# Routing on un-normed tokens, with the first expert's weights split before a branch, in a two-block float32 kernel

## The chip, the core and the metric

The kernel runs on one core of a Trainium2 chip. A core has TensorE (PE, matrix products; its weight loads are shown as PEld), VectorE (DVE), ScalarE (ACT), GpSimd (POOL) and SyncE (SP, which issues all the DMAs of this kernel). Each engine works through its own list of instructions in order and waits on semaphores for the others. The metric is the device time of one execution in microseconds (us).

## The reference, cut to what matters

A batch of one sequence of 256 tokens of 1024 float32 values goes through a mixer, a cross attention, a hierarchical mixture of experts (MoE), and then a second stack of two more layers. The change lies between the cross attention and the MoE:

```python
def rmsnorm(x, g):
    xf = x.astype(jnp.float32)
    y = xf * lax.rsqrt(jnp.mean(xf * xf, axis=-1, keepdims=True) + EPS)
    return (y * g.astype(jnp.float32)).astype(x.dtype)
...
    x = x + memory_cross_attention(...)          # ends with o @ w_xo
    x = x + hierarchical_moe(rmsnorm(x, norm_ffn_g[l]), w_rg[l], b_rg[l], w_re[l], b_re[l],
                             w_e_gate[l], w_e_up[l], w_e_down[l])
...
def hierarchical_moe(h, ...):
    p_grp = jax.nn.softmax(t @ w_rg + b_rg, axis=-1)      # 4 groups
    g_val, g_idx = lax.top_k(p_grp, 1)
    le = (t @ w_re + b_re).reshape(n, 4, 4)               # 4 experts in each group
    le_sel = jnp.take_along_axis(le, g_idx[:, :, None], axis=1)[:, 0]
    e_val, e_idx = lax.top_k(jax.nn.softmax(le_sel, axis=-1), 2)
    ...
    act = silu(einsum('nd,edf->nef', t, w_e_gate)) * einsum('nd,edf->nef', t, w_e_up)
    act = act * gate[:, :, None]
    out = einsum('nef,efd->nd', act, w_e_down)
```

Each of the 16 experts has a gate and an up matrix of 1024 x 256 and a down matrix of 256 x 1024.

## The kernel before

Activations lie feature-major: `xT` holds x as 128 partitions (features) x 8 feature tiles x 256 tokens. To keep float32 precision, each weight piece of 128 x 1024 values (512 KB, fetched by `wfetch`, L90, into one of 6 buffers `raw`) is split by `wsplit` (L96): ACT writes a rounded high part `whi` (L99) and DVE the remainder `wlo` (L100); activations have such pairs too (`hTh`/`hTl`, `xgh`/`xgl`). A product then is three matmuls: high by high, high by low, low by high (`mm_fm`, L141 to L143; `mm_tm`, L148 to L150). The split pairs sit in 6 buffers as well, and each is free again when TensorE has used it. PSUM has 8 banks, which `phase` (L58) shares out to kinds of tiles; `bank` (L69) takes one.

The order within an engine is not written out by hand: the recording layer places the instructions of each engine by its own estimate of time, with `fence`/`behind` as hints. Work that waits for another engine is written as generators; `later` queues one and `tick` moves each queued one a step on, after each block of 256 output columns.

The stretch that the change touches runs as follows. The output projection of the attention (`out_proj` with `w_xo`, L356) makes four column blocks of 48 matmuls, called xo blocks 0 to 3 here. After each, `resid` adds it to `xT` (DVE), and `norm.squares` squares it (ACT) and sums the squares over features by matmuls with a matrix of ones (L295). After block 3, `norm.finish` computes 1/rms for all 256 tokens on 128 x 256 values (L225 to L241), multiplies x by it and by the gain, and splits the result into `hTh`/`hTl` (L306 to L314, L217, L218). The router's logits are 24 matmuls over `hT` (L835 to L838). They are copied, transposed to tokens, and get their bias (L844). Then come `first_max` (L900) for the group, the rank of each token within its group by five small matmuls (L915 to L919), the `slot` of each token (L925 to L927), and `over`, which says whether any group has more than 128 tokens. `hT` is transposed to token-major `hMh`/`hMl` by 32 transposes (L936 to L947). `gating` (L952) computes the weights of the two chosen experts. `ada_mm` (L437) are small matmuls for a later layer, 4 for each 512 KB piece, and serve as filler; `ada_load` fetches those pieces.

Then stands a branch on `over` (L1101, L1102): when a group overflows, a whole second MoE pass runs. With these inputs it is skipped, but every engine loads the flag and branches. After the branch, `moe_pass` (L995) builds a 0/1 matrix `Pm` (token to slot, L999) and gathers each group's tokens by matmuls with it: `gather(0)` for groups 0 and 1 before the experts, then `gather(1)` for groups 2 and 3, each of 8 steps of 4 matmuls (L1011) with one ACT copy (L1013) and one DVE copy (L1014). The 16 experts follow, with up to three of them in flight: four pieces of gate and up, 24 matmuls (`gu`), a sigmoid, products on DVE, two transposes, two pieces of down, 12 matmuls (`py`); after every fourth expert a scatter back into `xT` (L1082, L1085). Three of expert 0's four pieces are fetched ahead of the branch (`pre`, L993) and split after it. SP, DVE and ACT are joined at the branch: what follows on one waits for the other's passing it.

Of the kernel before, what the change touches and what calls it, by code (L numbers as in the profile page):

```python
# [30 lines left out]
N_P = 3  # L31
# [8 lines left out]
def two_blocks_kernel(ctx, tc, A, out):  # L40
# [315 lines left out]
    def out_proj(aT, w2d, nx, gate=None, ws=(), ps0=None):  # L356

        for c in range(4):
# [6 lines left out]
            later(resid(c, ps, gate, nx))  # L365
# [133 lines left out]
    with tc.tile_pool(name="kv", bufs=1, reuse_waits="tile") as kvp:  # L499
# [265 lines left out]
        with tc.tile_pool(name="xa", bufs=2, reuse_waits="tile") as xp, tc.tile_pool(name="ad", bufs=B_X, reuse_waits="tile") as ad:  # L765
# [51 lines left out]

            skewed([head(h) for h in range(4)])
            nx = norm(g_ffn)
            wrt = xp.tile([P, KD, 20], F32, name="wrt", bufs=1)  # L820
# [3 lines left out]
            wrth = xp.tile([P, KD, 20], F32R, name="wrth", bufs=1)  # L824
            wrtl = xp.tile([P, KD, 20], F32R, name="wrtl", bufs=1)
            hilo(wrth, wrtl, wrt)
# [3 lines left out]
            out_proj(oT, A["w_xo"][0], nx)  # L830
            drain()
            hT = nx.finish()
            ada_mm(N_X)

            pl = bank("logits")  # L835
            for k in range(KD):
                mm_fm(pl[:20, :S], (wrth[:, k, :], wrtl[:, k, :]), hT, k, 0, k == 0, k == KD - 1, 20)
            lf = xp.tile([20, S], F32, name="lf", bufs=1)  # L838
            SC.activation(lf, pl[:20, :S], AF.Copy)
            pl = bank()  # L840
            for t in range(2):
                T.transpose(pl[:, 20 * t:20 * t + 20], lf[:, t * P:(t + 1) * P], ident[:20, :20])
            L = cp.tile([P, 2, 20], F32, name="L")
            V.tensor_tensor(L, pl[:, :40].rearrange("p (t c) -> p t c", t=2), bc(brt.unsqueeze(1), [2, 20]), op=OP.add)  # L844
# [36 lines left out]
    with (tc.tile_pool(name="ad3", bufs=5, reuse_waits="tile") as ad,  # L881
# [4 lines left out]
        for j in range(4):  # L886
            V.memset(w4[:, j:j + 1], float(4 - j))
            V.memset(b128[:, j:j + 1], float(128 * j))
# [11 lines left out]
        def first_max(l, nm):  # L900
# [8 lines left out]
            V.tensor_tensor(oh, oh, bc(r.unsqueeze(2), [2, 4]), op=OP.is_equal)  # L909
# [9 lines left out]
        T.matmul(pr[:, 8:12], ones, goh[:, 1, :], start=False, stop=True)  # L919
        rk = st([2, 4], "rk")  # L920
# [14 lines left out]

        hM = (mp.tile([P, 2, D], F32R, name="hMh"), mp.tile([P, 2, D], F32R, name="hMl"))  # L936
        for t in range(2):
            for c in range(2):
                for i in range(2):
                    ps = bank()  # L940
                    for j in range(4):
                        fence["T"] = T.transpose(ps[:, j * P:(j + 1) * P], hT[i][:, 4 * c + j, t * P:(t + 1) * P].bitcast(F32), ident)
                    dst = hM[i][:, t, 512 * c:512 * c + 512]
                    if i == 0:
                        SC.activation(dst, ps, AF.Copy)
                    else:
                        V.tensor_copy(dst, ps)  # L947

        drain()
        ada_step(N_R, ad)  # L950

        def gating():  # L952
# [27 lines left out]
            V.tensor_tensor(o1, o1, o2, op=OP.add)  # L980
            return o1


        def gate_up(E, kc):
            return [(lambda r, u=u: r.rearrange("p (k u f) -> p k u f", k=2, u=2)[:, :, u, :],
                     A[nm][0, E, kc * 256:kc * 256 + 256, :].rearrange("(k p) f -> p k f", p=P))
                    for u, nm in enumerate(("w_e_gate", "w_e_up"))]


        pre = []  # L990
        sqb = mp.tile([P, 2, CH], F32, tag="sq", name="pre")
        for kc in range(N_P):
            pre.append(wfetch(gate_up(0, kc), sqb[:, kc, :] if kc < 2 else ad.tile([P, CH], F32, tag="ada", name="pre")))  # L993

        def moe_pass(slot, okm, nx=None, pre=()):  # L995
# [39 lines left out]
            def expert(E):  # L1035
# [4 lines left out]
                for kc in range(4):  # L1040
                    hl = wsplit(pre[kc], CH) if E == 0 and kc < len(pre) else wload(gate_up(E, kc), CH)
                    for k in range(2):
                        wgu.append(tuple(w[:, k * 512:(k + 1) * 512] for w in hl))
# [666 lines left out]
```

## Time and profile before

| what | us |
|---|---|
| median of 3 runs (1231.42 to 1235.02) | 1234.59 |
| the profiled execution | 1230.13 |
| its span in the trace | 1228.1 |
| TensorE busy in the span | 1183.5 |
| VectorE busy | 888.9 |
| ScalarE busy | 696.2 |

The profiled execution is one run; 2.0 us of its time lie outside the span. A busy TensorE is not a TensorE at its peak: matmuls are counted as busy at a lower granted clock too. The granted clock is given as a share of full speed: 1.00 is 2.4 GHz and 0.50 is 1.2 GHz. Times within the span count from its start.

### The profile page before, as it was taken

What the parts mean: (1) busy time and instruction counts of PE and PEld (TensorE: products, weight loads), DVE (VectorE), ACT (ScalarE), POOL (GpSimd) and SP (SyncE); (2) the same over time, 40 slices, a digit from 0 to 9 for tenths busy, and PEclk for the clock granted to TensorE, in tenths of its full rate; (3) what the DMA queues carried; (4) which work ended last, traced back from release to release, by engine and by line L of the source; (5) the groups of instructions that cost most, each with busy time, mean ns of one, the idle gap of its engine ahead of it and who ended that gap; (6) DMA issues with size and microseconds to landing.
All of it is one profiled execution on the core that took longest, in us unless ns stands there. A gap on an engine that the chain in (4) does not pass through costs nothing.

```text
span 1228.1 us, 22512 instructions
## 1 busy us (share of the span) xinstructions
PE 1183.5 (96%) x8762; PEld 1061.1 (86%) x8762; DVE 888.9 (72%) x1672; ACT 696.2 (57%) x1163; POOL 26.6 (2%) x34
## 2 busy tenths in 40 slices
PE   7999999999879999899999999999999989999998
PEld 6989999989657888679757899999977768999998
DVE  7999977664468999888778595577489567654443
ACT  6644447553347887576457475555466455655543
POOL 0000000000000000070000000000000000000000
PEclk9999999999979999999999999999999999999999
DMA  7565575791357999786452597597656246656551
GB/s 240 199 218 185 163 222 174 248 320 58 124 176 256 330 354 350 278 254 206 124 186 92 190 379 250 183 325 267 221 210 191 85 138 207 227 186 190 188 172 35
DMA packets 177551, 257.76 MB, mean 210 GB/s; under 512 B 14239, under 2 KB 138999, under 8 KB 177436
## 3 DMA queue, kind: packets, MB, share of 16 engines
q1 hardware_dynamic: 177436, 256.24, 63.1%
q8 instruction: 71, 1.16, 0.4%
q14 instruction: 44, 0.36, 0.1%
HBM read 255.15 MB, written 1.05 MB: 209 GB/s over the span
## 4 chain that ended last, share of the span: by engine, by line
PE 64%; DVE 3%; ACT 2%; issue 1%; DMA 1%; ACTq 0%; DVEq 0%
PE fm L142 6%; PE fm L143 6%; PE fm L141 6%; PE mo L141 5%; PE mo L142 5%; PE mo L143 5%; PE tm L148 3%; PE tm L150 3%; PE tm L149 3%; PE gu L150 2%; PE gu L148 2%; PE gu L149 2%; PE ada L434 1%; PE o L1449 1%; PE py L148 1%
## 5 line engine op out<-in xcount | busy, mean ns | idle before, releaser
L100 DVE TENSOR_TENSOR wlo<-raw,whi 128x1024 fp32r<-128x1024 f32 (+1 forms) x382 | 455.3, 1213 | 168.0 <-ACT whi L99 163.7
L99 ACT ACTIVATE whi<-raw 128x1024 fp32r<-128x1024 f32 (+1 forms) x382 | 391.9, 1048 | 267.7 <-PE fm L142 139.0
L141 PE MATMUL fm<-hTh,whi 128*128 128x256 f32 (+1 forms) x968 | 272.8, 282 | 3.2 <-ACT hTh L217 3.2
L142 PE MATMUL fm<-hTl,whi 128*128 128x256 f32 (+1 forms) x968 | 272.8, 282 | 1.8 <-DVE hTl L551 0.7
L143 PE MATMUL fm<-hTh,wlo 128*128 128x256 f32 (+1 forms) x968 | 271.7, 281 | 0.8 <-DVE wlo L100 0.8
L141 PEld LDWEIGHTS fm<-hTh,whi 128*128 128x128 f32 (+1 forms) x968 | 182.2, 188 | 5.6 <-ACT hTh L217 4.6
L142 PEld LDWEIGHTS fm<-hTl,whi 128*128 128x128 f32 (+1 forms) x968 | 182.5, 189 | 4.0 <-DVE hTl L218 2.7
L143 PEld LDWEIGHTS fm<-hTh,wlo 128*128 128x128 f32 (+1 forms) x968 | 182.3, 188 | 1.1 <-DVE wlo L100 1.0
L142 PE MATMUL mo<-ul,whi 128*128 128x256 f32 x512 | 142.9, 280 | 0.0
L143 PE MATMUL mo<-uh,wlo 128*128 128x256 f32 x512 | 142.8, 280 | 0.0
L141 PE MATMUL mo<-uh,whi 128*128 128x256 f32 x512 | 141.7, 280 | 0.0
L143 PEld LDWEIGHTS mo<-uh,wlo 128*128 128x128 f32 x512 | 96.2, 188 | 0.0
L142 PEld LDWEIGHTS mo<-ul,whi 128*128 128x128 f32 x512 | 96.2, 188 | 0.0
L141 PEld LDWEIGHTS mo<-uh,whi 128*128 128x128 f32 x512 | 95.4, 188 | 0.4 <-issue 0.4
L148 PE MATMUL tm<-whi,hTh 128*128 128x512 f32 x176 | 69.4, 400 | 0.7 <-ACT hTh L217 0.7
L149 PE MATMUL tm<-wlo,hTh 128*128 128x512 f32 x176 | 69.0, 393 | 0.0
L150 PE MATMUL tm<-whi,hTl 128*128 128x512 f32 x176 | 68.0, 392 | 0.0
L142 PE MATMUL fm<-oTl,whi 128*128 128x256 f32 x192 | 54.4, 286 | 0.9 <-DVE oTl L1621 0.8
L141 PE MATMUL fm<-oTh,whi 128*128 128x256 f32 x192 | 53.1, 284 | 1.4 <-ACT oTh L1620 1.3
L143 PE MATMUL fm<-oTh,wlo 128*128 128x256 f32 x192 | 53.0, 280 | 0.0
L148 PE MATMUL gu<-whi,xgh 128*128 128x512 f32 x128 | 51.1, 401 | 1.8 <-ACT xgh L1013 1.8
L629 DVE SCALAR_TENSOR_TENSOR acv<-apad,chv,acv 128x256 f32<-128x256 f32 x120 | 51.4, 478 | 0.0
(523 smaller groups left out, 2136.9 us busy)
## 6 DMA issues: line engine op xcount, KB each, us to landing
ada<-in_w_ada_dram SPq DMA_DIRECT2D x96, 512.0 KB, 6.1
raw<-in_w_mlp_in_dram SPq DMA_DIRECT2D x64, 512.0 KB, 3.8
raw<-in_w_mlp_out_dram SPq DMA_DIRECT2D x64, 512.0 KB, 4.8
raw<-in_w_in_dram SPq DMA_DIRECT2D x48, 512.0 KB, 3.7
raw<-in_w_e_down_dram SPq DMA_DIRECT2D x32, 512.0 KB, 5.4
raw<-in_w_e_gate_dram SPq DMA_DIRECT2D x61, 256.0 KB, 5.2
raw<-in_w_e_up_dram SPq DMA_DIRECT2D x61, 256.0 KB
raw<-in_diff_w_in_dram SPq DMA_DIRECT2D x24, 512.0 KB, 4.1
```

The source lines that it names most:

```text
L99: behind("A", SC.activation(hi[:, :n], raw[:, :n], AF.Copy))
L100: last["lo"] = behind("V", V.tensor_tensor(lo[:, :n], raw[:, :n], hi[:, :n].bitcast(F32), op=OP.subtract))
L141: T.matmul(ps, whi[:, c:c + ncol], xh[:, xk, :], start=first, stop=False, **kw)
L142: T.matmul(ps, whi[:, c:c + ncol], xl[:, xk, :], start=False, stop=False, **kw)
L143: return T.matmul(ps, wlo[:, c:c + ncol], xh[:, xk, :], start=False, stop=last, **kw)
L148: T.matmul(ps, xh[:, xk, t0:t0 + P], w[0], start=first, stop=False)
L149: T.matmul(ps, xh[:, xk, t0:t0 + P], w[1], start=False, stop=False)
L150: return T.matmul(ps, xl[:, xk, t0:t0 + P], w[0], start=False, stop=last)
L434: behind("T", T.matmul(ada_part["ps"][32 * j:32 * j + 32, :], w, r[:, S * j:S * j + S], start=start, stop=stop, skip_group_check=True))
L629: V.scalar_tensor_tensor(acv[:, f, :], apad[:, f, j:j + S], chv[:, f, j:j + 1], acv[:, f, :], op0=OP.mult, op1=OP.add)
L1449: T.matmul(o_[64 * hp:64 * hp + 64, :], vTM[:, a, s, gi, :], PT[hp, s, a], start=s == 0 and a == 0, stop=False, skip_group_check=True)
```

## The change

- **Router on x instead of its norm.** The gain `norm_ffn_g` is multiplied into the router's weights (`wrt`, now 32 columns wide, plain float32 and not split). Logits, sums of squares and token-major copies of x are taken column block by column block in `resid_r`, one `tick` after each xo block. The 1/rms of a token is then one number per token in token-major form: `inv_rms` on 128 x 2 values, multiplied into the logits (`L`) and into the rows `xM` (x times the gain, token-major) to give `hMh` and `hMl`. The 32 transposes of `hT`, `norm.finish` and the split of the router's weights are gone.
- **Weights.** Expert 0's four pieces, and the high parts of expert 1's first two, are fetched and split ahead of the branch; twelve pieces in all are fetched ahead of it.
- **Order around the branch.** `Pm` is built ahead of the branch, `gating` behind it; 16 filler matmuls (`ada_mm(N_R)`) move behind it. The flag's load on DVE is put behind the last rows of `hMl`. The skip path is asked to be the one that the compare falls through to.
- **2 KB rows.** In a piece of gate and up, a partition now holds two neighbouring rows of the matrix (2 KB in one run) instead of two rows 128 apart (1 KB each); to match, the gather takes every second feature of 256 as a tile (`cs`).
- **Second gather.** The 8 steps of `gather(1)` are spread over experts 0 to 7, one in each.
- The overflow pass has its own weight buffers. Constants `w4` and `b128` are set on POOL.

```diff
-N_P = 3
+N_P = 2
...
+            def resid_r(c, ps, gate, nx):
+                xs = xT[:, 2 * c:2 * c + 2, :]
...
+                yield
+                for k in (2 * c, 2 * c + 1):
+                    T.matmul(lgb[:32, :S], wrt[:, k, :], xT[:, k, :], start=k == 0, stop=k == KD - 1)
+                pz = bank()
+                for f in range(2):
+                    for t in range(2):
+                        T.transpose(pz[:, (2 * t + f) * P:(2 * t + f + 1) * P], xs[:, f, t * P:(t + 1) * P], ident)
...
+                if c >= 2:
+                    for f in range(2):
+                        fence["T"] = T.matmul(ssb[32:64, :S], ones[:, :32], (sq if c == 3 else rq["qs"])[:, f, :],
+                                              start=c == 2 and f == 0, stop=c == 3 and f == 1)
+                V.tensor_tensor(xM[:, :, 256 * c:256 * c + 256], pz.rearrange("p (t d) -> p t d", t=2),
+                                bc(grow[:, 256 * c:256 * c + 256].unsqueeze(1), [2, S]), op=OP.mult)
+
+            out_proj(oT, A["w_xo"][0], None, res=resid_r)
+
+            pre = [wfetch(gate_up(i // 4, i % 4)) for i in range(6)]
+            split0 = [wsplit(r, CH) for r in pre[:4]]
+            pre += [wfetch(gate_up(i // 4, i % 4)) for i in range(6, 10)]
             drain()
-            hT = nx.finish()
-            ada_mm(N_X)
...
+            ada_mm(3)
...
+            rM = inv_rms(pl[:, :, 32], 2, 1.0 / D, "rM", cp)
             L = cp.tile([P, 2, 20], F32, name="L")
-            V.tensor_tensor(L, pl[:, :40].rearrange("p (t c) -> p t c", t=2), bc(brt.unsqueeze(1), [2, 20]), op=OP.add)
+            for t in range(2):
+                V.scalar_tensor_tensor(L[:, t, :], pl[:, t, 0:20], rM[:, t:t + 1], brt, op0=OP.mult, op1=OP.add)
+            ada_mm(N_X - 3)
...
+                SC.activation(hi, xm, AF.Copy, scale=rM[:, t:t + 1])
+
+        def rows_lo(t, c):
+            hi, lo = (v[:, t, 512 * c:512 * c + 512] for v in hM)
+            return V.scalar_tensor_tensor(lo, xM[:, t, 512 * c:512 * c + 512], rM[:, t:t + 1], hi.bitcast(F32),
+                                          op0=OP.mult, op1=OP.subtract)
...
-            gather(0)
+            for d in range(8):
+                gather(0, d)
+            o1, gated = gating()
+            if nx is not None:
+                ada_mm(N_R)
...
+                if E < 8:
+                    gather(1, E)
...
+        Pm, fence["H"] = places(slot, okm, "Pm")
+        for t in range(2):
+            Pm_ins = behind("H", rows_lo(t, 1))
...
-        with tc.If(flag > 0):
+        with tc.If(flag > 0, preferred_fallthrough_block=False):
```

How this moves TensorE's instructions between the last xo block and the branch: before, the sums of squares are followed by 32 filler matmuls, the logits from the normed `hT`, the ranks and the transposes of `hT`. Rows name the line, the operation, what is written and read, and the shape; xN is a repeat.

```order
L143 MATMUL fm<-oTh,wlo 128x256
L295 MATMUL ss<-qs,ones 128x256 x2
L295 MATMUL ss<-sq,ones 128x256 x2
L434 MATMUL ada<-ada,cond 32x256 x32
L141 MATMUL logits<-hTh,wrth 20x256
...
L842 MATMUL ax<-ident,lf 128x20 x2
L915 MATMUL rank<-go,tri 128x4
...
L942 MATMUL ax<-ident,hTh 128x128 x4
...
L434 MATMUL ada<-ada,cond 32x256
L1101 TENSOR_LOAD over
L1102 COMPARE_AND_BRANCH
```

Now, at the same place (the first row is the last matmul of xo block 3):

```order
L143 MATMUL fm<-oTh,wlo 128x256
L856 MATMUL logits<-xT,wrt 32x256 x2
L860 MATMUL ax<-ident,xT 128x128 x4
L867 MATMUL ss<-qs,ones 32x256 x2
L856 MATMUL logits<-xT,wrt 32x256
L860 MATMUL ax<-ident,xT 128x128 x2
...
L867 MATMUL ss<-sq,ones 32x256 x2
L434 MATMUL ada<-ada,cond 32x256 x12
L884 MATMUL ax<-ident,lf 128x64 x2
L434 MATMUL ada<-ada,cond 32x256 x20
L961 MATMUL rank<-go,tri 128x4
```

The logits and transposes of blocks 2 and 3 stand behind the last xo matmul; the same rows for blocks 0 and 1 stand ahead of it, behind blocks 1 and 2. Only `lf` (the logits and sums of squares, copied) and its two transposes lie between the sums and the ranks.

On DVE, from the last `go` (the chosen group) to the branch, the changed kernel has these rows:

```order
L955 TENSOR_TENSOR go<-go,gr 128x8
L976 SCALAR_TENSOR_TENSOR hMl<-xM,ir_y,hMh 128x512 x2
L982 TENSOR_TENSOR rk<-rank,go 128x8
...
L988 TENSOR_TENSOR slot<-slot,rnk 128x2
L491 SCALAR_TENSOR_TENSOR gA<-modc,gcols 128x8
L1038 TENSOR_SCALAR Pm<-slot_i,slot,okm 128x512 x2
L976 SCALAR_TENSOR_TENSOR hMl<-xM,ir_y,hMh 128x512 x2
L1191 TENSOR_TENSOR gfA<-gcols,gA 128x8
L1165 TENSOR_LOAD over
L1169 COMPARE_AND_BRANCH
L1169 UNCONDITIONAL_BRANCH
```

Before, the last rows there were copies of transposed `hT` and `modc`, and `Pm` stood behind the branch. Also a jump still stands right behind the compare.

On DVE right behind the branch, before (`wlo` are splits of weights, `xgl` the gather's copies; all of `gating` stands ahead of the branch):

```order
L491 SCALAR_TENSOR_TENSOR gA<-modc,gcols 128x8
L999 TENSOR_SCALAR Pm<-slot_i,slot,okm 128x512 x2
L1116 TENSOR_TENSOR gfA<-gcols,gA 128x8
L100 TENSOR_TENSOR wlo<-pre,whi 128x1024 x3
L1014 CAST xgl<-ax 128x256 x2
L100 TENSOR_TENSOR wlo<-raw,whi 128x1024 x3
L1014 CAST xgl<-ax 128x256 x2
```

And now, from the third copy of the gather on:

```order
L1025 TENSOR_TENSOR e2o<-e2o,e2m 128x8
L1058 CAST xgl<-ax 128x256
L1026 TENSOR_TENSOR e1o<-e1o,e2o 128x8
L100 TENSOR_TENSOR wlo<-raw,whi 128x1024 x2
L1058 CAST xgl<-ax 128x256
L100 TENSOR_TENSOR wlo<-raw,whi 128x1024
L1058 CAST xgl<-ax 128x256
L100 TENSOR_TENSOR wlo<-raw,whi 128x1024
L1058 CAST xgl<-ax 128x256
L100 TENSOR_TENSOR wlo<-raw,whi 128x1024 x2
L1058 CAST xgl<-ax 128x256 x2
```

The 26 small operations of `gating` and the first two copies stand ahead of these rows; no split of expert 0 is left among them, the first two here are expert 1's.

## Rows read from the trace of the kernel before

**Rows 1.** The page's first part: busy us, share of the span, instructions.

```profile
PE 1183.5 (96%) x8762; PEld 1061.1 (86%) x8762; DVE 888.9 (72%) x1672; ACT 696.2 (57%) x1163; POOL 26.6 (2%) x34
```

**Rows 2.** Windows: stretch, length, busy us of each engine (instructions), PEclk, DMA share, GB/s.

```profile
310.00:320.00 10.00, 10.00 (x87) 10.00 (x86) 5.41 (x7) 2.97 (x4) 0.00 (x0) 1.00 0.45 179
...
322.40:351.50 29.10, 21.34 (x176) 12.82 (x174) 15.53 (x69) 10.64 (x25) 0.00 (x0) 0.88 0.19 57
351.50:394.60 43.10, 37.94 (x188) 31.46 (x188) 35.87 (x49) 31.06 (x44) 0.00 (x0) 0.88 0.90 298
394.60:507.20 112.60, 112.60 (x527) 93.29 (x527) 106.28 (x129) 84.80 (x104) 0.00 (x0) 1.00 0.97 330
...
360.00:362.00 2.00, 2.00 (x8) 1.71 (x8) 1.81 (x3) 1.47 (x4) 0.00 (x0) 0.50 1.03 349
```

**Rows 3.** TensorE's timeline from xo block 3's end to the first gather.

```profile
322.41 1.02 PE L295 MATMUL ss<-qs,ones 128*128 128x256 f32 x4
...
324.60 3.66 PE L434 MATMUL ada<-ada,cond 128*32 128x256 f32 x64
...
337.90 0.36 PE L915 MATMUL rank<-go,tri 128*128 128x4 f32 x2 [1.38 <-DVE gv L960]
...
352.36 0.94 PE L1011 MATMUL ax<-Pm,hMh 128*128 128x256 f32 x3 [3.94 <-DVE Pm L999]
```

**Rows 4.** VectorE's timeline over the same stretch.

```profile
322.61 0.76 DVE L328 SCALAR_TENSOR_TENSOR xT<-fm,xT 128x256 f32<-128x256 f32 x2 [3.57 <-PE fm L143]
...
336.79 0.16 DVE L903 TENSOR_REDUCE gm<-L 128x2 f32<-128x8 f32 x1
...
339.76 0.16 DVE L921 TENSOR_TENSOR rk<-rank,go 128x8 f32<-128x8 f32 x1
...
340.66 0.15 DVE L927 TENSOR_TENSOR slot<-slot,rnk 128x2 f32<-128x2 f32 x1
...
347.91 0.17 DVE L475 TENSOR_TENSOR modc<-ax,bcol 128x8 f32<-128x8 f32 x1 [1.53 <-PE ax L472]
351.53 0.17 DVE L491 SCALAR_TENSOR_TENSOR gA<-modc,gcols 128x8 f32<-128x8 f32 x1 [3.46 <-DVEq L1102]
351.67 1.00 DVE L999 TENSOR_SCALAR Pm<-slot_i,slot,okm 128x512 fp32r<-128x512 f32 x2
```

**Rows 5.** ScalarE's timeline: last squares, first instruction behind the branch.

```profile
323.06 0.75 ACT L287 ACTIVATE sq<-xT 128x256 f32<-128x256 f32 x2 [4.75 <-DVE xT L328]
...
351.59 1.28 ACT L99 ACT_TABLE_LOAD   x1 [6.16 <-DVEq L1102]
```

**Rows 6.** The branch line L1102, sequencers: ns min/median/max, start us.

```profile
L1102 PEldq COMPARE_BRANCH x1: 3492/3492/3492, 346.6 to 346.6; - x1
L1102 DVEq COMPARE_BRANCH x1: 72/72/72, 348.5 to 348.5; - x1
...
L1102 DVEq EVENT_SEMAPHORE x1: 21/21/21, 351.4 to 351.4; - x1
```

**Rows 7.** TensorE's timeline behind the branch, experts 0 to 3.

```profile
356.15 0.79 PE L148 MATMUL gu<-whi,xgh 128*128 128x512 f32 x1 [1.77 <-ACT xgh L1013]
...
371.75 1.85 PE L1020 MATMUL ax<-e1o,Pm 128*128 128x4 f32 x16
...
374.01 0.60 PE L1029 MATMUL ax<-ident,Pm 128*128 128x128 f32 x4
...
376.74 0.39 PE L148 MATMUL gu<-whi,xgh 128*128 128x512 f32 x1
...
381.55 0.40 PE L1011 MATMUL ax<-Pm,hMh 128*128 128x256 f32 x2
```

**Rows 8.** VectorE's costliest group from 351.5 to 522, by form: busy, mean ns.

```profile
L100 DVE TENSOR_TENSOR wlo<-raw,whi 128x1024 fp32r<-128x1024 f32 x96 | 114.1, 1218 | 6.9 <-ACT whi L99 5.7
```

**Rows 9.** DMA issues of the gate matrices: KB each, median us to landing.

```profile
raw<-in_w_e_gate_dram SPq DMA_DIRECT2D x61, 256.0 KB, 5.2
```

**Rows 10.** SyncE's timeline: one issue of half a piece.

```profile
326.74 0.47 SPq L93 DMA_DIRECT2D pre<-in_w_e_up_dram  x1
```

More of the change, by code (lines that the diff above doesn't have):

```diff
@@ L364, in out_proj @@
             fence["D"] = last["w"]
-            later(resid(c, ps, gate, nx))
+            later((res or resid)(c, ps, gate, nx))
     phase(mm=4, ax=3)
@@ L829, in two_blocks_kernel @@
             nc.sync.dma_start(brt[:, 4:20], bcast_row(A["b_re"][0], 16))
-            out_proj(oT, A["w_xo"][0], nx)
-            drain()
-            hT = nx.finish()
-            ada_mm(N_X)
[L835 to L839, printed above, removed]
+            xM = act.tile([P, 2, D], F32, tag="aTh", name="xM")
@@ L919, in two_blocks_kernel @@
         T.matmul(pr[:, 8:12], ones, goh[:, 1, :], start=False, stop=True)
+        hM = (mp.tile([P, 2, D], F32R, name="hMh"), mp.tile([P, 2, D], F32R, name="hMl"))
+        for c in range(2):
+            for t in range(2):
+                hi = hM[0][:, t, 512 * c:512 * c + 512]
+                xm = xM[:, t, 512 * c:512 * c + 512]
+                SC.activation(hi, xm, AF.Copy, scale=rM[:, t:t + 1])
[3 more added lines that the diff above has]
+                                          op0=OP.mult, op1=OP.subtract)
+        for t in range(2):
+            behind("H", rows_lo(t, 0))
         rk = st([2, 4], "rk")
@@ L933, in two_blocks_kernel @@
         V.tensor_scalar(over, cmax, 128.0, None, op0=OP.is_gt)
[L936 to L950, printed above, removed]
+        ada_load(N_R, ad)
         def gating():
@@ L991, in two_blocks_kernel, with places @@
         sqb = mp.tile([P, 2, CH], F32, tag="sq", name="pre")
-        for kc in range(N_P):
-            pre.append(wfetch(gate_up(0, kc), sqb[:, kc, :] if kc < 2 else ad.tile([P, CH], F32, tag="ada", name="pre")))
-        def moe_pass(slot, okm, nx=None, pre=()):
-            Pm = mp.tile([P, 2, 512], F32R, tag="Pm", name="Pm")
+        for i in range(10, 10 + N_P):
+            pre.append(wfetch(gate_up(i // 4, i % 4), sqb[:, i - 10, :]))
+        def places(slot, okm, name):
+            Pm = mp.tile([P, 2, 512], F32R, name=name)
@@ L1097, in moe_pass @@
             skewed([expert(E) for E in range(16)])
-        o1 = gating()
-        flag = nc.values_load(over[0:1, 0:1], min_val=0, max_val=1)
-        with tc.If(flag > 0):
+        drain()
+        Pm, fence["H"] = places(slot, okm, "Pm")
+        for t in range(2):
+            Pm_ins = behind("H", rows_lo(t, 1))
+        loads, (flag,) = nc.values_load_multi_w_load_instructions(over[0:1, 0:1], min_val=0, max_val=1)
+        for ld in loads:
+            if ld.ins.engine == Pm_ins.ins.engine:
+                tc.add_manual_dep(ld.ins, Pm_ins.ins.name, NOSYNC, reason="behind the places")
+        with tc.If(flag > 0, preferred_fallthrough_block=False):
             sl2 = st([2], "sl2")
```

124 lines of the change are left out of this document (81 added, 43 removed).

## Prediction

> **What bounds the kernel now.** I read the engines' shares first: TensorE is busy for 96% of the span [rows 1], so only stretches where it idles or runs at a low clock can give much. The windows name two of them [rows 2]. From the end of xo block 3 (322.4) to the branch (351.5), 29.1 us hold 21.3 us of busy TensorE at a mean clock of 0.88, with DMA at 57 GB/s: nothing is bound there, it is a chain of small steps. From the branch to 394.6, TensorE is busy 37.9 of 43.1 us, again at 0.88. Behind that, to 507.2, it is busy for all of 112.6 us at full clock, while DVE is busy 106.3. So the MoE proper is TensorE's, and a time saved ahead of 394.6 is kept only if the work behind it starts earlier by as much; nothing there waits for a fixed moment.
>
> The timelines give the chain [rows 3 to 6]: block 3 is added on DVE at 322.61 and squared on ACT at 323.06, then come 1/rms, `hT` and the logits; the maximum of the group logits starts at 336.79, the ranks at 337.90, `rk` at 339.76, `slot` at 340.66. DVE's last instruction ahead of the branch, `modc`, ends at 348.08, its first behind it starts at 351.53. ACT's first one waits for DVE's passing, so DVE arrives last, and the branch costs 3.45 us from its arrival. `Pm` follows, and the first gather starts at 352.36.
>
> **The change, part by part.** All is counted from the profiled execution (1230.13; span 1228.1). The median is 4.46 above it; I add that at the end.
>
> *Ahead of block 3's end.* Behind blocks 1 and 2 stand two logits matmuls and four transposes each. Two plain float32 matmuls of 256 columns took 1.02 us [rows 3], four transposes 0.60 us from start to end [rows 7], of which about 0.4 keeps the next one off. That is 1.4 a set, 2.8 for two, since TensorE is full there (10.00 of 10) [rows 2]. The router's logits also hold one of the three banks that xo blocks used, so block 2 can no longer fill gaps between attention heads: 36 matmuls at 10/87 = 0.115 us [rows 2], between 0 and 4.1 us. Heads 2 and 3 keep two blocks as filler; I take 0.3, near the low end. Block 3 ends 3.1 later.
>
> The splits hoisted onto DVE and ACT there I cost at nothing: they lie under DVE's 5.4 and ACT's 3.0 of 10 us. They need weights that land 5.2 us after issue [rows 9] in buffers long free. One place could cost: two `whi` of expert 1 stand ahead of block 3's squares on ACT and wait for that block's own buffers. One ends late, 1.3 us behind the block, so the squares (0.75) [rows 5] are done 2.0 behind it. TensorE is then still busy with block 2's and 3's logits and transposes until 3.8, which covers it; without that cover it costs about 1.2.
>
> *From block 3's end to the branch.* In us behind it: logits and transposes of block 2 to 1.4, first sums 2.4, block 3's set 3.8, last sums 4.8, 12 filler matmuls (3.66 x 12/32 = 1.4) 6.2 [rows 3], two transposes 6.5. Then 1/rms on 128 x 2: five steps from the maximum to the ranks took 337.90 - 336.79 = 1.1 [rows 3, 4], so six steps cost 1.3 (7.8); bias and scale 0.3 (8.1); the group's maximum to the ranks 1.1 (9.2); the ranks to `rk` 1.86 before [rows 3, 4], at a mixed clock, 1.6 here (10.8). Two rows of `hMl` (0.6 each: half of a split's 1.22, [rows 8]) lie under the ranks. `rk` to the end of `slot` 1.05 [rows 4] (11.85), `modc` and `gA` 0.3 (12.15), `Pm` 1.0 [rows 4] (13.15), two more rows of `hMl` 1.25 (14.4), `gfA` 0.2 (14.6). The branch again 3.45: 18.05. So the branch ends at 322.41 + 3.1 + 18.05 = 343.6 in place of 351.5: **8.0 earlier**.
>
> SP has to be there too. Twenty-four issues of expert pieces stand ahead of the branch in place of six. Most go out under the xo blocks; the last eight (four filler loads, two pieces) may need space of the router's stretch, free by 8.1 at the latest, and at 0.47 each [rows 10] they end at 11.9, ahead of DVE's 14.6.
>
> The branch's price is the largest unknown. The nearest rows: DVE's own compare took 0.07 us, but its next event comes at 351.4, 2.9 later, and TensorE's compare took 3.49 [rows 6]. The skip path is now the one that falls through, yet the first row there is a jump over the same body. I take 3.45, and keep 0.6 as the low end (0.5 to load the flag, 0.07 to compare). The Trainium skill (Runtime: NRT & Kernel Launch, Instruction fetch mechanics) says that a taken branch to a target outside the fetched window must fetch it first. By that rule the jump that is left costs the same; the 2.9 us agree with it.
>
> *From the branch to the fourth expert.* Before, the 43.1 us hold this work of TensorE at full clock: 96 `gu` matmuls, 21 of them from 376.74 to 381.55 [rows 7], so 0.229 each, 22.0; 64 gather matmuls at 0.115, 7.4; the gate columns (L1020) 1.7; `Pm`'s transposes 0.7; experts' transposes 0.9; in sum 32.8. So 10.3 are lost: 0.8 for `Pm`, 1.8 until the first expert starts [rows 7], 0.5 a step later, some 4 to the low clock (0.50 at 360 to 362; a mean of 0.88 over 43.1 us makes 10.3 us at half rate, [rows 2]), the rest in the second gather, where its steps wait for DVE's copies.
>
> After: `Pm` is there and expert 0's splits are done. Still lost: 0.3 to the first gather; 0.3 until ACT, which loads its table (1.28, [rows 5]) and must do one exponential, copies the first step; 0.5 in other waits. TensorE again idled before the branch's end, so I take half rate for 5 us, 2.5 lost: half of before's 10.3, since the waits for the first expert's splits are gone (bounds: 0, and the 10.3 again, 5.2 lost). That is 3.6. The 16 filler matmuls that moved behind the branch add 1.8. 32.8 + 3.6 + 1.8 = 38.2 in place of 43.1: **4.9**. `gating`'s 26 small DVE operations (0.2 each, 5.2) lie beside the first gather steps; what hides them is that expert 0's splits (4 x 1.22) are no longer there.
>
> *Rest.* `gather(1)` spread: its gain is in the 10.3. Strided weight loads of the gather and 2 KB rows: nothing, since the trace shows no wait of TensorE for either. The skill (Perfetto Trace Analysis, DMA Optimizations) holds transfers under 2 KB to be costly, so the rule would have the MoE's DMA speed up. The trace differs in that DMA does not end the steps of 394.6 to 507.2, though its share is 0.97.
>
> Sum: 8.0 + 4.9 = 12.9; 1230.13 - 12.9 = 1217.2 for a profile, **1221.7** beside the median.
>
> **Rivals.**
> *A, forecast*: 8 to 18 us gained; 1216.6 to 1226.6. 0.60.
> *B, DVE takes the second term back.* Behind the branch the copies `xgl` alternate with splits, up to two in a row (2.44). Between the gather steps that wait for them TensorE has some 13 `gu` matmuls (3.0) against DVE's 2.44 + 0.42, so it decides once these waits are late by 0.2. At four places, 1.2 each, all of the 4.9 goes: gain 8.0, 1226.6; with the attention's filler lost too (3.8), 1230.4. 0.16.
> *C, more.* The branch falls to 0.6: 2.85 more, 1218.8. Or the MoE was DMA's after all, at its share of 0.97: then nine pieces more fetched ahead (4.7 MB at 330 GB/s, [rows 2]) give 14.3 in place of 4.9, 1212.3. In the sentence of the skill above, the 2 KB rows would add to this. Against it: TensorE has no gap there. 0.10.
> *D, no change.* The change starts the MoE earlier but TensorE stays at 1.2 GHz through experts 0 and 1, about 20 us of work in place of the 2.5 lost: at half rate a `gu` costs 0.43, so some 16 are lost, and 12.9 - 13.5 = -0.6: 1235. It needs low clock to about 36 us behind the branch, where before it held for about 10 [rows 2]. 0.08.
> *E, slower.* The same mechanism through experts 2 and 3, 11 us of work more: 9 lost, 1244. It decides from about 42 us of low clock on. For it: the new start interleaves gather and experts in small steps. Against it: before, that start had more waits, and the low clock held for about 10 us all the same. 0.06.
>
> **Numbers.** A measurement of this kernel tells 0.3%, 3.7 us, from no change. A, B and C are faster (0.86), D the same (0.08), E slower (0.06). The forecast is A's, 1221.7. The range goes from C's 1212 to B's 1231; outside lie D and E (0.14).
>
> **What would show it.** Right: block 3 ends near 325.5, DVE's first instruction behind the branch stands near 343.6, the first `gu` within 2.5 us of it, granted clock full some 6 us behind it, `gu` of expert 1 done within 21 us, and TensorE without gaps until the fourth expert; the MoE's end some 13 us earlier. Wrong: gaps between attention heads (filler), squares of block 3 waiting on ACT for `whi` beyond the logits, TensorE waiting for `xgl` behind pairs of splits, a branch that costs 0.6, or a clock that stays at 0.50.

## The result, and the profile after

The changed kernel took 1218.78 us (median of 4 runs, 1216.52 to 1220.45) against 1234.8 for the kernel before (4 runs, 1231.42 to 1237.4): a ratio of 0.9875, with a 95% interval of 0.9853 to 0.9897. The forecast was 1221.7. The profiled execution took 1216.52, its span 1214.6.

The engines' shares, against [rows 1], say little: TensorE's busy time fell by 6.2 us to 1177.3, and the span by 13.5.

The windows (columns as in [rows 2]) say where. The first runs from block 3's end to the first gather, the second from there to the end of the first expert's gate and up.

```profile
325.10:340.80 15.70, 10.43 (x103) 5.62 (x103) 9.20 (x33) 6.33 (x12) 1.09 (x10) 0.91 0.48 172
340.80:361.20 20.40, 20.34 (x128) 16.84 (x129) 15.82 (x44) 10.62 (x19) 0.00 (x0) 0.90 0.47 157
345.00:350.00 5.00, 5.00 (x28) 4.28 (x28) 4.86 (x16) 2.67 (x6) 0.00 (x0) 1.00 0.19 49
400.00:450.00 50.00, 50.00 (x240) 41.72 (x239) 47.84 (x57) 38.09 (x48) 0.00 (x0) 1.00 0.94 330
```

TensorE idles for 5.3 us ahead of the first gather, and for 0.06 behind it: the gaps of the old start are gone. The clock is full from 345 on, 4.2 us behind TensorE's restart.

TensorE's timeline, against [rows 3, 7]: the set of logits and transposes that stands behind block 2 (it is block 1's) up to the first matmul of block 3, the transposes of the logits between the filler, the ranks, the first gather, the first `gu`.

```profile
318.09 1.05 PE L856 MATMUL logits<-xT,wrt 128*32 128x256 f32 x4
...
319.48 0.36 PE L141 MATMUL fm<-oTh,whi 128*128 128x256 f32 x1
...
331.21 0.33 PE L884 MATMUL ax<-ident,lf 64*128 64x64 f32 x2
...
334.29 0.36 PE L961 MATMUL rank<-go,tri 128*128 128x4 f32 x2 [0.45 <-DVE go L955]
...
340.83 0.77 PE L1055 MATMUL ax<-Pm,hMh 128*128 128x256 f32 x2 [4.81 <-issue]
...
342.91 0.80 PE L148 MATMUL gu<-whi,xgh 128*128 128x512 f32 x1
```

VectorE's timeline, against [rows 4]. The first row is the kernel before's `over`, which the flag is loaded from; the others are the changed kernel's.

```profile
340.12 0.14 DVE L933 TENSOR_SCALAR over<-cmax 128x1 int32<-128x1 f32 x1
```

```profile
335.58 0.17 DVE L982 TENSOR_TENSOR rk<-rank,go 128x8 f32<-128x8 f32 x1
...
335.86 0.14 DVE L994 TENSOR_SCALAR over<-cmax 128x1 int32<-128x1 f32 x1
...
336.45 0.16 DVE L988 TENSOR_TENSOR slot<-slot,rnk 128x2 f32<-128x2 f32 x1
...
336.72 1.00 DVE L1038 TENSOR_SCALAR Pm<-slot_i,slot,okm 128x512 fp32r<-128x512 f32 x2
337.63 1.41 DVE L976 SCALAR_TENSOR_TENSOR hMl<-xM,ir_y,hMh 128x512 fp32r<-128x512 f32 x2
338.96 0.16 DVE L1191 TENSOR_TENSOR gfA<-gcols,gA 128x8 f32<-128x8 f32 x1
342.18 0.17 DVE L1001 TENSOR_TENSOR dg<-L,gm 128x8 f32<-128x8 f32 x1 [3.06 <-issue]
```

The line of the flag's load (L1165) and that of the branch (L1169) on the sequencers, against [rows 6] (ns min/median/max, start us): each engine now has a compare that falls through and a jump over the body, and all but POOL have a signal to the others between the two. PEldq and DVEq are the queues of TensorE and VectorE.

```profile
L1165 PEldq TENSOR_LOAD <-over x1: 488/488/488, 336.0 to 336.0; - x1
...
L1165 DVEq TENSOR_LOAD <-over x1: 541/541/541, 336.9 to 336.9; - x1
```

```profile
L1169 PEldq COMPARE_BRANCH  x2: 95/1910/3725, 336.6 to 336.9; - x2
L1169 DVEq COMPARE_BRANCH  x2: 51/53/55, 337.5 to 339.3; - x2
...
L1169 PEldq EVENT_SEMAPHORE  x1: 51/51/51, 336.8 to 336.8; - x1
L1169 DVEq EVENT_SEMAPHORE  x1: 21/21/21, 339.2 to 339.2; - x1
```

TensorE takes its jump from 336.9 to 340.7, while VectorE still makes `Pm` and `hMl`; VectorE signals at 339.2, and the gather starts 0.2 behind TensorE's own jump. VectorE's own first instruction comes 1.35 later.

To add the gain up, four marks are read in each trace: the first filler matmul (L434), which comes ahead of every edit of TensorE's work, the first gather, the first and last sigmoid (one for each expert), and the first sum of the next norm. First the kernel before, then the changed one (count, ns, first and last start).

```profile
L434 PE MATMUL ada<-ada,cond x576: 378/379/403, 254.2 to 1038.0; 128*32 128x256 f32 x192
...
L1011 PE MATMUL ax<-Pm,hMh x32: 277/283/583, 352.4 to 392.7; 128*128 128x256 f32 x32
...
L1048 ACT ACTIVATE sg<-gu x16: 363/385/405, 375.1 to 504.0; 128x256 f32<-128x256 f32 x16
...
L1094 PE MATMUL ss<-sq,gfe x16: 379/379/483, 520.0 to 524.2; 128*128 128x256 f32 x16
```

```profile
L434 PE MATMUL ada<-ada,cond x576: 379/379/637, 253.5 to 1025.3; 128*32 128x256 f32 x192
...
L1055 PE MATMUL ax<-Pm,hMh x32: 278/281/553, 340.8 to 426.5; 128*128 128x256 f32 x32
...
L1104 ACT ACTIVATE sg<-gu x16: 367/386/392, 361.2 to 487.8; 128x256 f32<-128x256 f32 x16
...
L1155 PE MATMUL ss<-sq,gfe x16: 379/379/379, 505.4 to 508.7; 128*128 128x256 f32 x16
```

Differences of these marks, in us, for all kernels of the study; for the changed kernel, 340.8 - 253.5 = 87.3, and so on. The last column is the ratio to the kernel before, which ran anew beside each set of runs.

```
                        first    gather to   1st to     last sg    first mark  ratio, 95% interval
                        gather   1st sg      last sg    to norm    to norm
before                   98.1     22.8       128.9       16.0       265.8      -
changed                  87.3     20.4       126.6       17.6       251.9      0.9875 (0.9853-0.9897)
e1_rows_1k               87.9     19.8       127.1       18.1       252.9      0.9893 (0.9872-0.9915)
e2_gather_at_once        87.4     20.6       131.7       18.3       258.0      0.9944 (0.9924-0.9964)
e3_splits_behind         87.4     20.4       126.4       18.4       252.6      0.9897 (0.9877-0.9918)
e4_four_pieces           87.1     20.6       126.3       18.4       252.4      0.9904 (0.9884-0.9924)
e5_no_branch             84.3     20.3       126.9       18.4       249.9      0.9865 (0.9838-0.9893)
e6_places_behind         89.0     21.4       126.2       18.4       255.0      0.9891 (0.9862-0.9920)
e7_gating_ahead          90.5     22.8       126.2       18.4       257.9      0.9932 (0.9908-0.9956)
e8_filler_moved          87.2     20.4       126.3       18.4       252.3      0.9907 (0.9888-0.9926)
e9_before_spread         99.2     22.9       127.4       19.4       268.9      1.0005 (0.9989-1.0022)
e10_fall_default         88.6     20.1       126.4       18.3       253.4      0.9908 (0.9893-0.9922)
e11_busy                 89.8     20.8       126.7       18.4       255.7      0.9932 (0.9915-0.9949)
e12_splits_behind2       87.8     27.3       126.3       18.1       259.5      0.9947 (0.9926-0.9967)
```

The gain stands ahead of the first sigmoid: 10.8 up to the first gather and 2.4 behind it. The 10.8 divide so: block 3 ends 3.4 later, `over` comes 6.9 sooner behind that end (10.8 in place of 17.7), and the gather 7.3 sooner behind `over` (5.0 in place of 12.2). No run takes the routing on un-normed x out by itself; its share of the 6.9 is read from the two traces alone. From there to the next norm both kernels need the same (144.9 and 144.2). By the next norm 13.9 us are won; behind it 1.1 go again (13.5 less of span, 0.7 of which the profiled run had already won ahead of the first mark). Both kernels have a gap of TensorE there (before, busy 5.27 of 8 us from 612 to 620, at full clock); in the changed kernel's trace the clock falls behind it (0.62 from 600 to 604, 0.53 from 604 to 608). A single profile does not tell whether that is the change's.

The runs of one kernel spread over some 4 to 11 us, so the marks tell experiments apart better than the medians. But each row is one profile, and two rows show what such a profile is worth. e9 has the same instructions in the same order as the kernel before up to the first gather, on TensorE, VectorE and ScalarE, and comes there 1.1 later. e3 came out as nearly the changed kernel (see there) and is 0.7 later at the norm: its clock fell to 0.50 ahead of the norm, and the changed kernel's did not. So differences of 1.1 or less are not read.

### The profile page after: what moved, and what is told of

Read it like the earlier page. It is cut to its first block, busy times and chain, and to the rows that moved or that the text cites. A ratio compares the mean times of both kernels' runs of the same rounds, so it can differ in the third digit from the quotient of the medians.

```text
span 1214.6 us, 22476 instructions
## 1 busy us (share of the span) xinstructions
PE 1177.3 (97%) x8738; PEld 1056.9 (87%) x8738; DVE 883.6 (73%) x1660; ACT 688.7 (57%) x1149; POOL 27.0 (2%) x43
## 4 chain that ended last, share of the span: by engine, by line
PE 65%; DVE 3%; ACT 1%; DMA 1%; issue 1%; SPq 0%; ACTq 0%; DVEq 0%
PE fm L142 6%; PE fm L143 6%; PE fm L141 6%; PE mo L141 5%; PE mo L142 5%; PE mo L143 5%; PE tm L148 3%; PE tm L150 3%; PE tm L149 3%; PE gu L148 2%; PE gu L150 2%; PE gu L149 2%; PE ada L434 1%; PE o L1524 1%; PE py L148 1%; PE py L150 1%
```

## The experiments

All but e9 start from the changed kernel.

**The branch. e10: without the option on the compare.**

```diff
-        with tc.If(flag > 0, preferred_fallthrough_block=False):
+        with tc.If(flag > 0):
```

> The changed kernel without the option of the branch: the jump over the body is again the compare's own, in place of a compare that falls through and a jump behind it. The prediction costed this part of the change at nothing. My theory: with the option, DVE's signal to the others comes ahead of its jump (339.2), so TensorE and ScalarE wait only for their own; without it DVE's signal comes behind its fetch, 2.9 us later, and the first gather is 1.2 to 1.5 us later (TensorE's own jump ends at 340.7 and covers the rest): 1219.5 to 1221. Rival (the prediction's): no difference, within 0.3 of the first gather's moment.

The first gather came 1.3 later, and the next norm 1.5; my theory holds in its mechanism, though its size is little above the noise. VectorE's signal now stands behind its jump, at 342.8, and TensorE waits for it (branch line, then TensorE's timeline):

```profile
L1169 PEldq COMPARE_BRANCH  x1: 4713/4713/4713, 337.5 to 337.5; - x1
...
L1169 DVEq COMPARE_BRANCH  x1: 72/72/72, 338.4 to 338.4; - x1
...
L1169 DVEq EVENT_SEMAPHORE  x1: 21/21/21, 342.8 to 342.8; - x1
```

```profile
342.97 0.77 PE L1055 MATMUL ax<-Pm,hMh 128*128 128x256 f32 x2 [6.09 <-DVEq L1169]
```

TensorE's own jump took 4.7 here, which alone would have given 0.7 of the 1.3, and 3.4 to 4.3 in the other variants. Over all runs the account is simple. In eight (the changed kernel, e1 to e4, e8, e11, e12) TensorE's own jump ends last, and the gather starts 0.16 to 0.22 behind its end, though the jump's length differs; in e7 and e10 it starts 0.2 behind VectorE's signal.

The traces also show what the length goes with. The page lists a DMA queue of the kind "instruction" (packets, MB, share):

```profile
q8 instruction: 70, 1.15, 0.4%
```

In each of the 13 kernels with a branch, one packet of this queue (16 KB) falls into TensorE's jump. It starts 1.0 to 2.25 us behind the jump's start (2.25 in e10), takes 0.9 to 1.4, and the jump ends 1.3 to 1.4 behind its end. In e5, which has no branch, there is none between 336.6 and 352.0. What delays the packet's start stays open.

**e6: the places behind the branch.**

```diff
-        Pm, fence["H"] = places(slot, okm, "Pm")
...
         fence.clear()
+        Pm, _ = places(slot, okm, "Pm")
```

> The changed kernel with the places (Pm, 1.0 us of DVE) behind the branch in place of ahead of it. The prediction's account (all engines restart when DVE has passed): the restart is 1.0 earlier, Pm comes behind it, and the first gather and the time stay (within 0.5 us). My theory now (TensorE restarts by itself, 3.7 us behind its own flag, at the same moment as DVE's last low rows): the gather waits for DVE's restart and Pm, 1.4 us later at least, and the time is 1 to 3 us more, 1220 to 1222.

The gather came 1.7 later and the next norm 3.1, but this does not show what `Pm` ahead of the branch is worth. Without `Pm` and its fence, all four rows of `hMl` stand ahead of `over`, where the changed kernel has two. So `over` (339.07 in this trace) came 1.1 later, counted from the first mark, TensorE's jump started as much later, and it took 4.3 in place of 3.7: together the 1.7. It ended at 344.5, and the gather starts 0.2 behind it, as in the changed kernel; the first half of `Pm`, behind VectorE's restart at 343.90, is done at about the same moment. The row names `Pm` only as what ended last.

```profile
336.21 2.07 DVE L976 SCALAR_TENSOR_TENSOR hMl<-xM,ir_y,hMh 128x512 fp32r<-128x512 f32 x3
...
343.90 1.00 DVE L1038 TENSOR_SCALAR Pm<-slot_i,slot,okm 128x512 fp32r<-128x512 f32 x2 [4.01 <-issue]
```

```profile
L1168 PEldq COMPARE_BRANCH  x2: 95/2210/4325, 339.8 to 340.1; - x2
```

```profile
344.63 0.98 PE L1055 MATMUL ax<-Pm,hMh 128*128 128x256 f32 x3 [6.48 <-DVE Pm L1038]
```

**e5: no branch.** The diff takes out the flag's load and the whole `tc.If` body.

> The changed kernel without the branch: the pass for tokens beyond 128 in a group is left out, with the flag and the jump. My theory: what is left of the gap ahead of the gather is the branch's; the first gather then starts when the places and the first half of the low rows are there, 3.0 us earlier (337.8 in the clock of the changed kernel's trace in place of 340.8), TensorE's low clock behind it is shorter, and 3 to 5 us come off: 1214 to 1216. Rival (the branch costs 0.6, the rest of the gap is the chain): 1 us or less.

The gather came 3.0 earlier, as expected, and now waits for `Pm`; but only 2.0 of that reach the next norm, less than the 3 to 5 of my theory, and the time is not told from the changed kernel's. The gates' operations also moved ahead here. TensorE still falls to the low clock (from 340.4 to 343.8), though it idled for 1.73 us only ahead of the gather and was busy for 2.78 of the 5 us from 335 to 340 (window and timeline):

```profile
340.00:345.00 5.00, 4.88 (x21) 4.06 (x20) 4.76 (x19) 1.71 (x6) 0.00 (x0) 0.66 0.01 5
```

```profile
339.00 0.77 PE L1055 MATMUL ax<-Pm,hMh 128*128 128x256 f32 x3 [1.73 <-DVE Pm L1038]
```

**e11: TensorE kept at work up to the branch.**

```diff
-            T.transpose(pz[:, m * P:(m + 1) * P], row[:, m * P:(m + 1) * P], ident)
+            fence["Z"] = T.transpose(pz[:, m * P:(m + 1) * P], row[:, m * P:(m + 1) * P], ident)
...
         drain()
+        pad = bank("py")
+        for i in range(4):
+            ins = T.matmul(pad, ones, slot_i, start=True, stop=True)
+            tc.add_manual_dep(ins.ins, fence["Z"].ins.name, NOSYNC, reason="behind the ranks")
```

> The changed kernel with four float32 matmuls of 512 columns (about 1.0 us each), whose result nobody reads, on TensorE between the ranks and the branch. It measures what the low clock behind the branch costs, and whether TensorE can work while it takes the jump. My theory: DVE went through its own flag with 2.4 us of work still in its queue, so TensorE may too; then the first gather stays at its moment, the clock is full behind the branch in place of half for 4.2 us, and 2 us come off: 1216 to 1217. Rival 1 (TensorE does not come to its flag before the matmuls are done): the first gather is 3 to 4 us later, with full clock, and 1 to 2 us are lost, 1220 to 1221. Rival 2 (the gathers and first gu wait for copies, and the clock there costs nothing): no change though the clock is full.

None fits whole. The gather came 2.5 later, so TensorE does not work through its jump: the four matmuls end at 344.86, its signal goes at 344.9, and the jump, from 345.0 to 348.5, stands behind it (the releaser in the row is only what ended last by then). And the clock fell all the same, in the 3.8 us of the jump: at 350 to 355 it was 0.50. The added work bought nothing, and 3.8 were lost by the next norm.

```profile
L1173 PEldq COMPARE_BRANCH  x2: 95/1755/3415, 342.0 to 345.0; - x2
...
L1173 PEldq EVENT_SEMAPHORE  x1: 51/51/51, 344.9 to 344.9; - x1
```

```profile
341.26 3.60 PE L1164 MATMUL py<-slot_i,ones 128*128 128x512 f32 x8
348.63 0.76 PE L1055 MATMUL ax<-Pm,hMh 128*128 128x256 f32 x2 [3.77 <-DVE gs L1004]
```

**e8: filler out of the chain.**

```diff
-            ada_mm(3)
+            ada_mm(1)
...
+        ada_mm(2)
         rk = st([2, 4], "rk")
```

> The changed kernel with one of the three filler steps (4 matmuls each, 0.115) ahead of the transposes of the logits in place of three, the two others behind with the rest. In the changed kernel's trace the logits' copies end at 330.44 and the transposes start at 331.21, behind the filler. My theory (the way from block 3 to the gather is one chain, so each step taken out of it moves the gather): the first gather 0.7 us earlier, counted from a moment ahead of the change, and 0.5 to 0.8 off the time, 1218.0 to 1218.3, which only the trace can tell. Rival (the filler is only moved: its eight matmuls delay the ranks by as much): the first gather where it was.

The rival: the first gather stood where it was, within the noise. From the first mark the transposes came 0.6 sooner, but the filler then stood ahead of the ranks, which came 0.3 sooner, as did TensorE's jump, which took 0.1 longer.

**The gates. e7: ahead of the branch, as before.**

```diff
-            o1, gated = gating()
...
+        o1, gated = gating()
         drain()
         Pm, fence["H"] = places(slot, okm, "Pm")
```

> The changed kernel with the 26 small DVE operations of the gates ahead of the branch, as they stood before. My theory: DVE arrives at the branch some 3 us later (they are mixed with the chain of the ranks, the flag is 0.5 to 1 later too), restarts 3 us later, and the first copies of the gather are late by as much: 2 to 4 us lost, 1221 to 1223. Rival (DVE's work is only moved, and TensorE has the same to wait for): within 1 us of 1218.8.

More than my theory: 3.2 later at the gather, 2.4 more to the first sigmoid, 6.0 at the next norm. VectorE's signal came at 344.8, since two splits of expert 1 also moved in ahead of the branch, and TensorE waited for it 3.4 us beyond its own jump. Of the 3.2 these splits are 2.4, so the run does not price the gates alone. Behind the gather ScalarE's table load (1.28), which the changed kernel has ahead of it, came at 346.26; TensorE waited 0.96 for `xgh`, and the clock was 0.50 until 353.4.

```profile
L1169 PEldq COMPARE_BRANCH  x2: 95/1730/3365, 337.9 to 338.2; - x2
...
L1169 DVEq EVENT_SEMAPHORE  x1: 21/21/21, 344.8 to 344.8; - x1
```

```profile
344.99 0.77 PE L1055 MATMUL ax<-Pm,hMh 128*128 128x256 f32 x2 [7.88 <-DVEq L1169]
```

**The weights ahead. e3 and e4** took out splits and pieces:

```diff
-            split0 = [wsplit(r, CH) for r in pre[:4]]
-            pre += [wfetch(gate_up(i // 4, i % 4)) for i in range(6, 10)]
+            split0 = []
```

> The changed kernel with the first expert's four splits behind the branch (eight pieces fetched ahead of it in place of twelve). My theory: DVE then has 26 small operations (5.2), eight copies (3.4) and four splits (4.9) between 342.2 and the last gu of the first expert; TensorE waits for it 3 to 5 us, and the half clock lasts longer: 1222 to 1225. Rival (the gain is the earlier branch and the fetched weights; splits are hidden behind the gather): within 1 us of 1218.8.

In e4, `pre` ends at four pieces, and the two in `sqb` go.

> The changed kernel with the first expert's four pieces fetched and split ahead of the branch as now, and none of the next eight. My theory: the pieces of expert 1 are issued from 340.3 on and land before TensorE is done with expert 0, so 0 to 2 us are lost: 1219 to 1221. Rival (the MoE is bound by its transfers): eight pieces of 0.5 MB less ahead at 330 GB/s are 12.7 us of transfer, less the 7 us in which SP was idle behind the branch: 5 us or more lost, 1224 or above.

Both were within 0.7 of the changed kernel at the next norm, but neither tested what it was meant to. The recording layer moves a fetch or a split into any free buffer: e3 still had all twelve pieces ahead of the branch and e4 ten, and both the same four splits on VectorE. So e3 is the changed kernel with other buffers. (The expectation of e12 says six splits and ten pieces for both: six is right for the high parts on ScalarE, four for the low parts on VectorE; ten pieces is right for e4 alone.) What e4 does show is that the last two pieces ahead are worth nothing that these marks can tell.

**e12** has e3's edit too, and holds the splits where the others only named them:

```diff
+            split0 = []
...
+                c0 = SC.activation(xg[gp][0][:, d, :], ps[:, 0:S], AF.Copy)
+                c1 = V.tensor_copy(xg[gp][1][:, d, :], ps[:, S:2 * S])
+                if gp == d == 0:
+                    fence["A"], fence["V"] = c0, c1
```

> The changed kernel with every split of the experts' weights held behind the first copies of the gather, and eight pieces fetched ahead of the branch. In the two runs before that took out splits or pieces, six splits and ten pieces stood ahead of the branch all the same, since the program moves what has a free buffer; here the splits can't move. My theory (with the gates' small operations behind the branch, DVE needs the time that the splits ahead leave it): four splits (4.9 us of DVE) must end before the first expert does, TensorE waits for them 3 to 5 us, the first expert ends 23 to 25 us behind the first gather in place of 20.4, and the time is 1222 to 1225. Rival (the splits are hidden behind gathers and gates): within 1 us of the 20.4, and of the time.

The first expert took 27.3 us from the first gather, 6.9 more than in the changed kernel and more than my theory. TensorE waits twice for a copy `xgl` (4.3 in sum), and the low clock lasts until about 358, 13.5 us in place of 4.2; TensorE's work in it costs an estimated 2.6 more than in the changed kernel (half of its busy time at the low clock, 9.2 against 4.1), which makes up the 6.9. Only the second copy stands behind splits on VectorE, four of them. Ahead of the first there is none: ScalarE makes six high parts in a row, and VectorE idles 1.78 us until one of these, by the profile, lets it go on. (Timelines of TensorE, ScalarE and VectorE, then a window.)

```profile
349.30 0.80 PE L1054 MATMUL ax<-Pm,hMh 128*128 128x256 f32 x2 [2.77 <-DVE xgl L1057]
354.97 0.80 PE L1054 MATMUL ax<-Pm,hMh 128*128 128x256 f32 x2 [1.53 <-DVE xgl L1057]
```

```profile
346.06 5.78 ACT L99 ACTIVATE whi<-raw 128x1024 fp32r<-128x1024 f32 x6
```

```profile
347.81 0.16 DVE L1003 TENSOR_REDUCE gs<-dg 128x2 f32<-128x8 f32 x1 [1.78 <-ACT whi L99]
```

```profile
350.00:355.00 5.00, 3.47 (x10) 1.87 (x9) 5.00 (x10) 2.47 (x5) 0.00 (x0) 0.50 0.56 154
```

**The second gather. e2: its steps together, ahead of the first expert in the code.**

```diff
+            for d in range(8):
+                gather(1, d)
...
-                if E < 8:
-                    gather(1, E)
```

> The changed kernel with the eight steps of the second gather together, ahead of the first expert, as before. My theory: TensorE then waits at some of these steps for DVE's copies (0.42 each, with splits of 1.22 between), 1 to 3 us in sum, and the time is 1220 to 1222. Rival (the spread gather is the whole second term): 4 to 5 us lost, 1223 to 1224. Other rival (the copies are hidden anyway): within 0.5 of 1218.8.

6.1 us more at the next norm, above every theory. TensorE waited 2.3 us for `xgl`; then its clock fell, and the transfers stopped (share 0.45, then 0.00 to 390). That the splits' buffers were held by the waiting TensorE is only argued:

```profile
378.00:382.00 4.00, 1.69 (x12) 1.30 (x11) 2.83 (x6) 1.76 (x5) 0.00 (x0) 0.90 0.96 352
382.00:386.00 4.00, 3.53 (x12) 2.63 (x13) 1.87 (x5) 1.04 (x3) 0.00 (x0) 0.50 0.45 170
386.00:390.00 4.00, 4.00 (x16) 3.25 (x16) 2.47 (x4) 2.61 (x4) 0.00 (x0) 0.75 0.00 0
```

**e9: the kernel before, with the spread alone.** The diff is e2's, turned round, in the kernel before.

> The kernel of before with one edit of the change: the second gather's eight steps spread over experts 0 to 7. My theory: the spread by itself takes away the three waits of TensorE at 389 to 394 (2.0 us in sum) and the stop of the transfers behind them: 2 to 4 us off the time of before, 1229 to 1231. Rival (the spread helps only where the first expert's splits are done): within 1 us of before's 1233.

No gain in time: the interval leaves 1.4 us at most. The waits did go (TensorE was busy for all of 385 to 400), with 1.5 less between the sigmoids, but the gather was 1.1 later, ahead of the edit, and 3.4 more went behind the last sigmoid. There TensorE idled 4.6 in place of 3.5, and its clock was 0.50 for a part, where it stayed full in the kernel before; that this comes from the spread is not shown. In the kernel before, the same gap (390 to 394, TensorE busy 2.23 of 4.00) came with the clock at 1.00, so the spread had less to save.

**e1: 1 KB rows.**

```diff
-        r.rearrange("p (u k f) -> p u k f", k=2, u=2)[:, u]
+        r.rearrange("p (k u f) -> p k u f", k=2, u=2)[:, :, u, :]
...
-                cs = slice(256 * (d // 2) + d % 2, 256 * (d // 2) + 256, 2)
+                cs = slice(P * d, P * d + P)
```

> The changed kernel with gate and up in rows of 1 KB again (and the tokens' columns contiguous in the gather). My theory: the MoE is TensorE's, its transfers are hidden, so the time stays within 2 us of 1218.8, and the first stretch behind the branch looks the same. Rival (the MoE is bound by its transfers, whose share was 0.97): the 16,000 packets come back, TensorE waits for pieces between experts 4 and 12, and the time is 3 us or more above 1218.8.

1.0 more at the next norm, which is not told from noise, and no waits for pieces; the intervals overlap. The theory stands. The DMA share from 400 to 450 is 0.99 in place of 0.94 at the same rate: in that stretch a packet of 2 KB took 84 ns (median) in the changed kernel, one of 1 KB 46 ns here. So longer rows do make a transfer cheaper, as the Trainium skill says (Perfetto Trace Analysis, DMA Optimizations), and nothing here waits for that.

```profile
400.00:450.00 50.00, 50.00 (x241) 41.73 (x241) 47.81 (x60) 38.87 (x51) 0.00 (x0) 1.00 0.99 331
```

No variant that computes everything beat the changed kernel.

## Why the prediction was right, point by point

- **Block 3's end.** Forecast 3.1 later: 2.7 by the trace's clock, 3.4 from the first mark. A set took 319.48 - 318.09 = 1.39, against 1.4. The squares ended at 326.82, 1.7 behind the block, under TensorE's work.
- **The chain to the branch.** Step by step behind block 3 (325.10): ranks 9.2 (forecast 9.2), `rk` 10.5 (10.8), `slot` 11.5 (11.85), `Pm` 12.6 (13.15), `gfA` 14.0 (14.6). Right, a little long.
- **The branch: the step that failed in form.** I added one price of 3.45 to VectorE's arrival and 0.3 to the first gather. VectorE's restart fits (3.06; 342.18 in place of 343.6). But TensorE pays its own jump, under VectorE's last 2.2 us of work, and needs of VectorE only a signal. So the first gather came 10.8 earlier, not 352.36 - 343.9 = 8.5. The option, costed at nothing, is 0.8 to 1.5 of that: in e10 the gather stands 88.6 behind the first mark, against 87.1 to 87.9 in the runs in which TensorE's own jump decides and the flag comes as in the changed kernel. What `Pm` ahead of the branch gives, counted as 0.8, no run prices (e6).
- **Behind the first gather.** 12.9 - 8.5 = 4.4 was forecast, 3.1 measured to the next norm. The low clock lasted 4.2 us, forecast 5: 2.1 lost in place of 2.5. TensorE never waited for `xgl`. The 3.1 is 2.4 to the first sigmoid and 2.3 between the sigmoids, less 1.6 behind the last one.
- **What hides the gates.** That expert 0's splits have to be out of VectorE's way was right in kind: held together behind the first copies, they cost 6.9 (e12). But 2.8 of the 4.3 us of waits there came with ScalarE's half of the splits, which the forecast did not name, and no run puts them back where the kernel before had them. The spread, which I counted within the 10.3 and gave no price, is worth 6.1 here and, in the kernel before, 1.5 between the sigmoids and nothing in the time. These parts do not add: each one left out costs more than the 3.1 of the whole second term.
- **2 KB rows, strided weights.** Costed at nothing: e1's 1.0 is within the noise.
- **Rivals.** B's mechanism is real (copies `xgl` late behind splits: the second wait of e12, the waits of e2), but the change takes away what sets it off. C: the branch still costs 3 us (e5), and the MoE does not wait for transfers. D and E: the clock was full at 345.0.

So the mechanisms of the forecast were right, except for the way in which TensorE restarts. Its sum (12.9, against 13.9 by the next norm) is good in part by luck: the first term was 2.3 too small, the second 1.3 too large.

## What to carry to other kernels

Read a branch engine by engine: each takes its own jump when its own work is done, so the engine that restarts the bottleneck should reach it early, and whatever the others must tell it should stand ahead of their jumps. When TensorE starts on a new stage, look at what VectorE and ScalarE must copy for it, and clear these queues of large operations first; parts that each do this cannot be priced alone, only by leaving each out of the whole. Where a scheduler moves instructions, check in the order of the engines that an experiment took out what it names.

## What was not expected of the hardware

- A jump over the skipped body holds TensorE for 3.4 to 4.7 us and leaves VectorE idle for 3.0 to 3.5 (4.0 in e6, with the flag's load in it), though a compare that falls through takes 0.1. The Trainium skill (Runtime: NRT & Kernel Launch, Instruction fetch mechanics) holds that a taken branch beyond the fetched window must be fetched; the traces agree, with one 16 KB packet of the instruction queue inside each of TensorE's jumps and none in e5, and they add that the engines pay it side by side.
- VectorE's sequencer loaded its flag at 336.9, with 2.2 us of its own work still to be done, but its signal, and TensorE's in e11, came only when that work was done.
- TensorE's clock fell to 0.50 behind an idle time of 1.73 us in e5 (busy for 2.78 of the 5 us from 335 to 340), and behind 3.8 in e11, where TensorE had been busy for 4.82 of the 5 us from 340 to 345. In the kernel before it stayed at 1.00 with TensorE busy 2.23 of the 4 us from 390 to 394.
